# Rotary embedding on one core: cos and sin loaded by SyncE into 32 partitions and spread by TensorE

## The chip, the core and the metric

The kernel runs on one core of one Trainium2 chip. The metric is the device time of one execution in microseconds, as the median over runs. The core's engines are TensorE (PE; its weight loads are PEld), VectorE (DVE), ScalarE (ACT), GpSimd (POOL) and SyncE (SP). Sixteen DMA engines move the data. ScalarE issues DMAs on one hardware queue (q10 in the profile) and SyncE on another (q1).

## What is computed

```python
batch, seq, dim = (16, 512, 1024); num_heads = 16      # head_dim 64, half_dim 32
x = x.reshape(batch, seq, num_heads, head_dim)
x1, x2 = x[..., :half_dim], x[..., half_dim:]
cos = cos[None, :, None, :]; sin = sin[None, :, None, :]    # each (512, 32) float32
out = concatenate([x1 * cos - x2 * sin, x1 * sin + x2 * cos], axis=-1)
```

Everything is float32. x and the output are 33.55 MB each, and each of the two tables is 64 KB.

## The kernel before, in words

**Tiles.** The sixteen batches are cut into ten tiles. Batches 0, 1, 14 and 15 are "singles": partition s holds the sequence rows 4s to 4s+3, 16 KB (R1 = 4). The other twelve go in six pairs: a batch lies in 64 partitions of 8 rows each, 32 KB (R2 = 8). A "row" u is one sequence position per partition, 128 x 1024 elements; there are 64 of them. `x_sb` is a ring of 40 rows; a result is written over its x and stored from there.

**Tables.** A single needs cos and sin with partition s holding positions 4s to 4s+3; a pair needs partition p holding eight positions of its own batch, a different layout. Before, ScalarE issues the loads of both tables (L174) right after the first x load; each is 128 partitions by 512 B and lands in `stage`. From there three things are made. VectorE copies cos to PSUM (L264, `c1_ps`). ScalarE writes sine with both signs to `s1_sb` (L182, L183). For the pairs ScalarE makes a selection matrix `pick` from the identity (L177), two TensorE matmuls with it spread both tables into `pair_ps` (L208), and ScalarE writes signed sine from there to `s2_sb` (L186, L187); VectorE keeps signed sine of one row in PSUM (L271, L272).

**A row's work.** GpSimd multiplies the row, halves swapped, with signed sine into `t2_sb` (L257); for one row in eight of a pair tile VectorE does that instead (L286). VectorE multiplies the row with cos into one of three PSUM slots (L293). The sum is made by VectorE (L304), or, for the rows marked `PE2`, by TensorE adding `t2` through the identity into the PSUM slot (L224), after which ScalarE copies it back (L191). GpSimd also builds the identity at the start (L235, L237); VectorE and TensorE zero the PSUM slots first (L262, L201).

**Order.** Each engine runs a list written out by hand, with semaphores between the lists. ScalarE issues all x loads: those of the first 40 rows at once, later ones between its copies, each after the store that frees its place in the ring (line 194). SyncE issues the stores, a tile at a time (L161). GpSimd's first multiplication waits for `sem_s` (signed sine) and for the first tile; VectorE's first waits for cos, the zeroing and the first tile. Before the pair tiles (`(t, r) == (2, 0)`, row 8) both wait for the second count of `sem_s`.

Of the kernel before, what the change touches and what calls it, by code (L numbers as in the profile page):

```python
# [6 lines left out]
def bass_split_heads_rope_kernel(  # L7
# [18 lines left out]
    HD = dim // H  # L26
    HALF = HD // 2
    P = 128
    R1 = seq // P
# [3 lines left out]
    fp32 = mybir.dt.float32  # L33
# [3 lines left out]
    COPY = mybir.ActivationFunctionType.Copy  # L37
# [24 lines left out]
    NT2 = 6  # L62
    BANK = 512
    EH = H * HD // BANK
    LEAD = 1
    LAG = 10

    with ExitStack() as stack:
        x_sb = stack.enter_context(nc.sbuf_tensor([P, RING, H, 2, HALF], fp32))
        t2_sb = stack.enter_context(nc.sbuf_tensor([P, NT2, H, 2, HALF], fp32))  # L70
        stage = stack.enter_context(nc.sbuf_tensor([P, 2, R1 * HALF], fp32))
        s1_sb = stack.enter_context(nc.sbuf_tensor([P, R1, 2, HALF], fp32))
        s2_sb = stack.enter_context(nc.sbuf_tensor([P, R2, 2, HALF], fp32))
        ident = stack.enter_context(nc.sbuf_tensor([P, P], fp32))
        pick = stack.enter_context(nc.sbuf_tensor([P, 2, P // 2, 2], fp32))
        zero = stack.enter_context(nc.sbuf_tensor([P, BANK], bf16))
        tab_ps = stack.enter_context(nc.psum_tensor([P, BANK], fp32))
        pair_ps = stack.enter_context(nc.psum_tensor([P, 2, 2, R1, HALF], fp32))
# [4 lines left out]
        sem_cos = stack.enter_context(nc.semaphore("cos"))  # L83
        sem_sin = stack.enter_context(nc.semaphore("sin"))
        sem_c = stack.enter_context(nc.semaphore("ctab"))
        sem_s = stack.enter_context(nc.semaphore("stab"))
        sem_z = stack.enter_context(nc.semaphore("zero"))
        sem_i = stack.enter_context(nc.semaphore("ident"))
# [6 lines left out]
        sem_t = stack.enter_context(nc.semaphore("pairs"))  # L95
        sem_a = stack.enter_context(nc.semaphore("act"))

        c1_ps = tab_ps[:, 0:R1 * HALF].rearrange("p (r d) -> p r d", d=HALF)
        v_ps = tab_ps[:, R1 * HALF:R1 * HALF + HD].rearrange("p (t d) -> p t d", d=HALF)

        def c_of(t, r):
            return c1_ps[:, r, :] if tiles[t][1] == R1 else pair_ps[:, r // R1, 0, r % R1, :]
# [50 lines left out]
            eng.dma_start(in_sbuf(t), in_dram(x1, x2, t)).then_inc(sem_in[t], 16)  # L153

        def on_sync(sp):
            for u in range(NU):
                t, r, k = where(u)
                if r == tiles[t][1] - 1:
                    wait_added(sp, u)
                    k = u // R2  # L160
                    sp.dma_start(in_dram(o1, o2, t), in_sbuf(t)).then_inc(sem_out[k] if k < EARLY else sem_rest, 16)  # L161
            sp.wait_ge(sem_rest, 16 * sum(stores_of(k) for k in range(EARLY, NU // R2)))

        def on_scalar(ae):
            later = {}
            for t, (b, n) in enumerate(tiles):
                if b * R1 + n <= RING:
                    load(ae, t)
                else:

                    later.setdefault((b * R1 - RING) // R2 * R2 + R2 - 1 + LAG, []).append(t)
                if t == 0:
                    for i, (table, sem) in enumerate(((cos, sem_cos), (sin, sem_sin))):
                        ae.dma_start(stage[:, i, :], table.rearrange("(s r) d -> s (r d)", r=R1)).then_inc(sem, 16)  # L174

            ae.wait_ge(sem_i, 2)
            ae.activation(  # L177
                pick[:], ident[:].rearrange("q (s k) -> q k s", k=2)[:, :, :, None].broadcast_to([P, 2, P // 2, 2]), COPY
            ).then_inc(sem_g, 1)
            ae.wait_ge(sem_sin, 16)  # L180
            sv = stage[:, 1, :].rearrange("s (r d) -> s r d", d=HALF)
            ae.activation(s1_sb[:, :, 0, :], sv, COPY, scale=-1.0)  # L182
            ae.activation(s1_sb[:, :, 1, :], sv, COPY).then_inc(sem_s, 1)  # L183
            ae.wait_ge(sem_t, 2)
            s2 = s2_sb[:].rearrange("p (k r) t d -> p k r t d", r=R1)
            ae.activation(s2[:, :, :, 0, :], pair_ps[:, :, 1, :, :], COPY, scale=-1.0)  # L186
            ae.activation(s2[:, :, :, 1, :], pair_ps[:, :, 1, :, :], COPY).then_inc(sem_s, 1)  # L187
            for u in range(NU):
                if PE2[u]:
                    ae.wait_ge(sem_e, n_pe[u])  # L190
                    ae.activation(xs[:, u % RING, :], t1_ps[:, u % NT1, :], COPY).then_inc(sem_a, 1)  # L191
                for t in later.get(u, ()):
                    k = (tiles[t][0] * R1 - RING) // R2
                    ae.wait_ge(sem_out[k], 16 * stores_of(k))
                    load(ae, t)

        def on_tensor(pe):
            pe.wait_ge(sem_z, 1)
            for k in range(NT1):
                for b in range(EH):  # L200
                    pe.matmul(  # L201
                        t1_ps[:, k, b * BANK:(b + 1) * BANK], zero[:, 0:P], zero[:], start=True, stop=True
                    ).then_inc(sem_w, 1)
            pe.wait_ge(sem_g, 1)
            pe.wait_ge(sem_cos, 16)
            pe.wait_ge(sem_sin, 16)
            for k in range(2):
                pe.matmul(  # L208
                    pair_ps[:, k].rearrange("p c r d -> p (c r d)"),
                    pick[:, k].rearrange("q s b -> q (s b)"),  # L210
                    stage[:].rearrange("q c f -> q (c f)"),
                    start=True,
                    stop=True,
                ).then_inc(sem_t, 1)
            for u in range(NU):
                if not PE2[u]:
                    continue
                pe.wait_ge(sem_m, u + 1)

                if not V2[u]:  # L220
                    pe.wait_ge(sem_p, n_pool[u])
                t2 = t2_sb[:, u % NT2, :, :, :].rearrange("p h t d -> p (h t d)")
                for b in range(EH):
                    ins = pe.matmul(  # L224
                        t1_ps[:, u % NT1, b * BANK:(b + 1) * BANK],
                        ident[:],
                        t2[:, b * BANK:(b + 1) * BANK],
                        start=False,
                        stop=True,
                        skip_group_check=True,  # L230
                    )
                ins.then_inc(sem_e, 1)

        def on_gpsimd(pl):
            pl.memset(ident[:], 1.0).then_inc(sem_i, 1)  # L235
            pl.wait_ge(sem_i, 1)
            pl.affine_select(  # L237
                out=ident[:],
                in_=ident[:],
                compare_op=mybir.AluOpType.is_equal,  # L240
                fill=0.0,
                base=0,
                pattern=[[-1, P]],
                channel_multiplier=1,
            ).then_inc(sem_i, 1)
            for u in range(NU):
                if V2[u]:
                    continue
                t, r, k = where(u)
                if (t, r) == (0, 0):  # L250
                    pl.wait_ge(sem_s, 1)
                if (t, r) == (2, 0):
                    pl.wait_ge(sem_s, 2)
                if r == 0:
                    pl.wait_ge(sem_in[t], 16)
                wait_t2_free(pl, u)
                pl.tensor_tensor(  # L257
                    t2_sb[:, u % NT2, :, :, :], swapped(k), over_heads(s_of(t, r)), mult
                ).then_inc(sem_p, 1)

        def on_vector(ve):
            ve.memset(zero[:], 0.0).then_inc(sem_z, 1)  # L262
            ve.wait_ge(sem_cos, 16)
            ve.tensor_copy(c1_ps, stage[:, 0, :].rearrange("s (r d) -> s r d", d=HALF)).then_inc(sem_c, 1)  # L264
            ve.wait_ge(sem_c, 1)
            ve.wait_ge(sem_w, NT1 * EH)

            def pair_tables():
# [7 lines left out]
            def mul(u):  # L276
                t, r, k = where(u)
                if r == 0:
                    ve.wait_ge(sem_in[t], 16)
                if (t, r) == (2, 0):  # L280
                    pair_tables()
                if u == first_v:
                    ve.wait_ge(sem_c, 3)
                if V2[u]:
                    wait_t2_free(ve, u)
                    ve.tensor_tensor(t2_sb[:, u % NT2, :, :, :], swapped(k), over_heads(v_ps), mult)  # L286
                if u >= NT1:
                    v = u - NT1
                    if PE2[v]:
                        ve.wait_ge(sem_a, n_pe[v])  # L290
                    else:
                        ve.wait_ge(sem_v, n_comb[v])
                ve.tensor_tensor(  # L293
                    t1_ps[:, u % NT1, :].rearrange("p (h d) -> p h d", d=HALF),
                    x_sb[:, k, :, :, :].rearrange("p h t d -> p (h t) d"),
                    c_of(t, r)[:, None, :].broadcast_to([P, 2 * H, HALF]),
                    mult,
                ).then_inc(sem_m, 1)
# [56 lines left out]
```

## Time and profile before

| What | Value |
|---|---|
| Runs (median of 3) | 161.54 us (161.30 to 161.64) |
| Profiled execution, first to last instruction (span) | 160.3 us |
| Median of the runs less that span | 1.2 us |
| Busy: GpSimd, VectorE, TensorE, ScalarE | 134.9, 130.3, 72.8, 24.4 us |
| DMA: bytes, mean rate over the span | 67.26 MB, 419 GB/s |
| Tables: issue to landing, cos and sin | 7.8 and 7.5 us |
| First x load: issue, issue to landing | 0.81 us, 8.0 us |
| First multiplications: VectorE, GpSimd | 9.37 us, 9.85 us |

For the profiled execution no time is given beside its span; what lies around the span is taken as the difference in the third row. How to read the views: the page's slices cut the span in 40 parts, each digit a busy share in tenths. A queue's share is the time that its packets took, out of 16 engines over the stretch asked for; it can pass 100% when packets overlap or run past the stretch, since a packet counts where it starts. The chain lists start, length and what was waited for; the list of waits has engine and operation, what it waited for, total, times and longest.

### The profile page before, as it was taken

The numbers are of one execution on the slowest core, as the hardware profiler recorded it, in microseconds if no ns is written. First come the engines' busy times: TensorE is split into PE (matmuls) and PEld (weight loads), VectorE is DVE, ScalarE is ACT, GpSimd is POOL, SyncE is SP. The second block draws the span as 40 slices with busy tenths as digits, with TensorE's granted clock in tenths as the row PEclk, the third lists the DMA queues.
The fourth block names the chain that finished last, engine by engine and source line by source line (L and its number), as shares of the span: only waits on it lengthen the run. The fifth ranks groups of instructions, "written<-read, shape, count | busy, mean of one in ns | idle before, by whom it ended". The sixth has DMA issues, their size and how long they took to land.

```text
span 160.3 us, 522 instructions
## 1 busy us (share of the span) xinstructions
PE 72.8 (45%) x94; PEld 24.0 (15%) x94; DVE 130.3 (81%) x117; ACT 24.4 (15%) x27; POOL 134.9 (84%) x64
## 2 busy tenths in 40 slices
PE   6050004478357936660847105489458435850000
PEld 1020002022202211210221002022202111220000
DVE  0069998599989999996999709899889999999500
ACT  0420000203120222022012010201220402040000
POOL 1059999999999999999999999699999999289400
PEclk9955555557755587689687965555555977699555
DMA  5999999999999999999999999999999999999896
GB/s 147 409 441 474 409 450 409 425 429 429 446 429 458 417 411 466 409 433 401 450 433 425 425 409 458 409 433 433 411 429 462 441 417 401 450 441 441 376 450 294
DMA packets 3170, 67.26 MB, mean 419 GB/s; under 512 B 352, under 2 KB 608, under 8 KB 608
## 3 DMA queue, kind: packets, MB, share of 16 engines
q10 hardware_dynamic: 1728, 33.69, 49.6%
q1 hardware_dynamic: 1440, 33.56, 48.9%
q14 instruction: 2, 0.02, 0.0%
HBM read 33.69 MB, written 33.55 MB: 419 GB/s over the span
## 4 chain that ended last, share of the span: by engine, by line
DMA 60%; POOL 13%; DVE 8%; PE 7%; issue 3%; ACT 2%; ACTq 1%; DVEq 0%
DMA x_sb<-in_x_dram 41%; DMA out_dram<-x_sb 18%; POOL t_sb L257 13%; PE t_ps L224 7%; DVE t_ps L293 5%; DVE x_sb L304 3%; ACT x_sb L191 2%; ACTq L153 1%; ACTq L174 1%; DVE t_sb L286 0%; DVEq L303 0%
## 5 line engine op out<-in xcount | busy, mean ns | idle before, releaser
L257 POOL TENSOR_TENSOR t_sb<-x_sb,s_sb 128x1024 f32<-128x1024 f32 x58 | 134.2, 2346 | 14.8 <-ACT s_sb L183 8.5
L224 PE MATMUL t_ps<-t_sb,ident 128*128 128x512 f32 x84 | 68.0, 957 | 63.0 <-DVE t_ps L293 39.2
L293 DVE TENSOR_TENSOR t_ps<-x_sb,pair_ps 128x1024 f32<-128x1024 f32 x48 | 57.7, 1223 | 9.9 <-ACT x_sb L191 9.8
L304 DVE TENSOR_TENSOR x_sb<-t_ps,t_sb 128x1024 f32<-128x1024 f32 x43 | 52.4, 1218 | 2.6 <-POOL t_sb L257 2.6
L224 PEld LDWEIGHTS t_ps<-t_sb,ident 128*128 128x128 f32 x84 | 22.1, 290 | 108.9 <-DVE t_ps L293 74.6
L191 ACT ACTIVATE x_sb<-t_ps 128x1024 f32<-128x1024 f32 x21 | 21.5, 1023 | 109.9 <-PE t_ps L224 96.9
L293 DVE TENSOR_TENSOR t_ps<-x_sb,tab_ps 128x1024 f32<-128x1024 f32 x16 | 19.3, 1222 | 0.1
L286 DVE TENSOR_TENSOR t_sb<-x_sb,tab_ps 128x1024 f32<-128x1024 f32 x6 | 7.3, 1213 | 0.0
L264 DVE COPY tab_ps<-stage 128x128 f32<-128x128 f32 x1 | 0.3, 294 | 7.8 <-DMA stage<-in_cos_dram 7.8
L208 PE MATMUL pair_ps<-stage,pick 128*128 128x256 f32 x4 | 2.0, 667 | 5.4 <-DMA stage<-in_sin_dram 5.4
L201 PE MATMUL t_ps<-zero 128*128 128x512 bf16 x6 | 2.7, 627 | 1.3 <-DVE zero L262 1.3
L208 PEld LDWEIGHTS pair_ps<-stage,pick 128*128 128x128 f32 x4 | 1.2, 324 | 6.4 <-issue 6.3
L177 ACT ACT_TABLE_LOAD x1 | 1.3, 1283 | 5.5 <-issue 5.5
L201 PEld LDWEIGHTS t_ps<-zero 128*128 128x128 bf16 x6 | 0.7, 136 | 2.4 <-DVE zero L262 1.2
L262 DVE MEMSET zero<- 128x256 uint32 x1 | 0.3, 272 | 0.9 <-PEq L337 0.9
L186 ACT ACTIVATE s_sb<-pair_ps 128x256 f32<-128x256 f32 x1 | 0.4, 383 | 1.7 <-PE pair_ps L208 1.7
L182 ACT ACTIVATE s_sb<-stage 128x128 f32<-128x128 f32 x1 | 0.3, 309 | 2.1 <-DMA stage<-in_sin_dram 2.1
L235 POOL MEMSET ident<- 128x128 f32 x1 | 0.2, 204 | 0.3 <-POOLq L337 0.3
L177 ACT ACTIVATE pick<-ident 128x256 f32<-128x256 f32 x1 | 0.4, 416 | 0.0
L187 ACT ACTIVATE s_sb<-pair_ps 128x256 f32<-128x256 f32 x1 | 0.4, 379 | 0.0
L237 POOL TENSOR_SCALAR_AFFINE_SELECT ident<-ident 128x128 f32<-128x128 f32 x1 | 0.3, 292 | 0.1
L337 POOL MEMSET const-float32-0.0<- 128x1 f32 x1 | 0.1, 98 | 0.3 <-issue 0.3
(6 smaller groups left out, 1.0 us busy)
## 6 DMA issues: line engine op xcount, KB each, us to landing
x_sb<-in_x_dram ACTq DMA_DIRECT2D x6, 4096.0 KB, 38.0
out_dram<-x_sb SPq DMA_DIRECT2D x6, 4096.0 KB, 25.0
x_sb<-in_x_dram ACTq DMA_DIRECT2D x4, 2048.0 KB, 22.6
out_dram<-x_sb SPq DMA_DIRECT2D x4, 2048.0 KB, 15.2
stage<-in_cos_dram ACTq DMA_DIRECT2D x1, 64.0 KB, 7.8
stage<-in_sin_dram ACTq DMA_DIRECT2D x1, 64.0 KB, 7.5
```

The costliest lines, as they stand in the source:

```text
L153: eng.dma_start(in_sbuf(t), in_dram(x1, x2, t)).then_inc(sem_in[t], 16)
L174: ae.dma_start(stage[:, i, :], table.rearrange("(s r) d -> s (r d)", r=R1)).then_inc(sem, 16)
L177: ae.activation(pick[:], ident[:].rearrange("q (s k) -> q k s", k=2)[:, :, :, None].broadcast_to([P, 2, P // 2, 2]), COPY).then_inc(sem_g, 1)
L186: ae.activation(s2[:, :, :, 0, :], pair_ps[:, :, 1, :, :], COPY, scale=-1.0)
L191: ae.activation(xs[:, u % RING, :], t1_ps[:, u % NT1, :], COPY).then_inc(sem_a, 1)
L201: pe.matmul(t1_ps[:, k, b * BANK:(b + 1) * BANK], zero[:, 0:P], zero[:], start=True, stop=True).then_inc(sem_w, 1)
L208: pe.matmul(pair_ps[:, k].rearrange("p c r d -> p (c r d)"), pick[:, k].rearrange("q s b -> q (s b)"), stage[:].rearrange("q c f -> q (c f)"),
L224: ins = pe.matmul(t1_ps[:, u % NT1, b * BANK:(b + 1) * BANK], ident[:], t2[:, b * BANK:(b + 1) * BANK], start=False, stop=True, skip_group ...
L257: pl.tensor_tensor(t2_sb[:, u % NT2, :, :, :], swapped(k), over_heads(s_of(t, r)), mult).then_inc(sem_p, 1)
L286: ve.tensor_tensor(t2_sb[:, u % NT2, :, :, :], swapped(k), over_heads(v_ps), mult)
L293: ve.tensor_tensor(t1_ps[:, u % NT1, :].rearrange("p (h d) -> p h d", d=HALF), x_sb[:, k, :, :, :].rearrange("p h t d -> p (h t) d"), c_of ...
L304: ve.tensor_tensor(xs[:, k, :], t1_ps[:, u % NT1, :], t2_sb[:, u % NT2, :, :, :].rearrange("p h t d -> p (h t d)"), add,).then_inc(sem_v, 1)
```

## The change

SyncE's list now begins with the loads of both tables, each into 32 partitions with 2 KB (sixteen positions) per partition; ScalarE no longer issues them. GpSimd builds two sets of selection matrices at the start, `pick1` (32 x 4 x 128) and `pick2` (32 x 2 x 128), with a memset and an affine selection each; these stand ahead of the identity's own selection, which is kept. TensorE spreads the tables by matmuls over 32 rows: four, accumulated, put cos and sin for the singles side by side in the PSUM bank `tab_ps`; two and two do the same for the pairs into `pair_ps` (TQ = 32, TJ = 4, TI = 2, NF = R1 * HALF = 128). VectorE's copy of cos and ScalarE's making of `pick` are gone. ScalarE reads sine for the singles from PSUM, after the new semaphore `sem_f`. VectorE's first work waits for the first count of `sem_s`, which covers the cos table as well, instead of for cos.

```diff
-        stage = stack.enter_context(nc.sbuf_tensor([P, 2, R1 * HALF], fp32))
+        stage = stack.enter_context(nc.sbuf_tensor([TQ, 2, TJ, R1 * HALF], fp32))
-        pick = stack.enter_context(nc.sbuf_tensor([P, 2, P // 2, 2], fp32))
+        pick1 = stack.enter_context(nc.sbuf_tensor([TQ, TJ, P], fp32))
+        pick2 = stack.enter_context(nc.sbuf_tensor([TQ, TI, P // 2, 2], fp32))
...
         def on_sync(sp):
+            for i, (table, sem) in enumerate(((cos, sem_cos), (sin, sem_sin))):
+                sp.dma_start(
+                    stage[:, i].rearrange("q j f -> q (j f)"), table.rearrange("(q n) d -> q (n d)", q=TQ)
+                ).then_inc(sem, 16)
...
         def on_scalar(ae):
-                if t == 0:
-                    for i, (table, sem) in enumerate(((cos, sem_cos), (sin, sem_sin))):
-                        ae.dma_start(stage[:, i, :], table.rearrange("(s r) d -> s (r d)", r=R1)).then_inc(sem, 16)
-
-            ae.wait_ge(sem_i, 2)
-            ae.activation(
-                pick[:], ident[:].rearrange("q (s k) -> q k s", k=2)[:, :, :, None].broadcast_to([P, 2, P // 2, 2]), COPY
-            ).then_inc(sem_g, 1)
-            ae.wait_ge(sem_sin, 16)
-            sv = stage[:, 1, :].rearrange("s (r d) -> s r d", d=HALF)
-            ae.activation(s1_sb[:, :, 0, :], sv, COPY, scale=-1.0)
-            ae.activation(s1_sb[:, :, 1, :], sv, COPY).then_inc(sem_s, 1)
+            ae.wait_ge(sem_f, 1)
+            ae.activation(s1_sb[:, :, 0, :], sin1_ps, COPY, scale=-1.0)
+            ae.activation(s1_sb[:, :, 1, :], sin1_ps, COPY).then_inc(sem_s, 1)
...
         def on_tensor(pe):
-            pe.wait_ge(sem_g, 1)
+            pe.wait_ge(sem_g, 4)
             pe.wait_ge(sem_cos, 16)
             pe.wait_ge(sem_sin, 16)
+            for j in range(TJ):
+                ins = pe.matmul(
+                    tab_ps[:, 0:2 * NF].rearrange("p (c f) -> p c f", c=2),
+                    pick1[:, j],
+                    stage[:, :, j, :],
+                    start=j == 0,
+                    stop=j == TJ - 1,
+                )
+            ins.then_inc(sem_f, 1)
             for k in range(2):
-                pe.matmul(
-                    pair_ps[:, k].rearrange("p c r d -> p (c r d)"),
-                    pick[:, k].rearrange("q s b -> q (s b)"),
-                    stage[:].rearrange("q c f -> q (c f)"),
-                    start=True,
-                    stop=True,
-                ).then_inc(sem_t, 1)
+                for i in range(TI):
+                    ins = pe.matmul(
+                        pair_ps[:, k].rearrange("p c r d -> p c (r d)"),
+                        pick2[:, i].rearrange("q s b -> q (s b)"),
+                        stage[:, :, 2 * i + k, :],
+                        start=i == 0,
+                        stop=i == TI - 1,
+                    )
+                ins.then_inc(sem_t, 1)
...
         def on_gpsimd(pl):
+            pl.memset(pick1[:], 1.0).then_inc(sem_g, 1)
+            pl.memset(pick2[:], 1.0).then_inc(sem_g, 1)
             pl.memset(ident[:], 1.0).then_inc(sem_i, 1)
+            pl.wait_ge(sem_g, 2)
+            pl.affine_select(
+                out=pick1[:],
...
+                pattern=[[-1, TJ], [1, P]],
+                channel_multiplier=-TJ,
+            ).then_inc(sem_g, 1)
+            pl.affine_select(
+                out=pick2[:],
...
+                pattern=[[-1, TI], [1, P // 2], [0, 2]],
+                channel_multiplier=-TI,
+            ).then_inc(sem_g, 1)
             pl.wait_ge(sem_i, 1)
...
         def on_vector(ve):
             ve.memset(zero[:], 0.0).then_inc(sem_z, 1)
-            ve.wait_ge(sem_cos, 16)
-            ve.tensor_copy(c1_ps, stage[:, 0, :].rearrange("s (r d) -> s r d", d=HALF)).then_inc(sem_c, 1)
-            ve.wait_ge(sem_c, 1)
+            ve.wait_ge(sem_s, 1)
             ve.wait_ge(sem_w, NT1 * EH)
...
-                    ve.wait_ge(sem_c, 3)
+                    ve.wait_ge(sem_c, 2)
```

More of the change, by code (lines that the diff above doesn't have):

```diff
@@ L64, in bass_split_heads_rope_kernel @@
     EH = H * HD // BANK
+    TQ = 32
+    TJ = P // TQ
+    TI = TJ // 2
     LEAD = 1
@@ L85, in bass_split_heads_rope_kernel @@
         sem_c = stack.enter_context(nc.semaphore("ctab"))
+        sem_f = stack.enter_context(nc.semaphore("firsttab"))
         sem_s = stack.enter_context(nc.semaphore("stab"))
@@ L96, in bass_split_heads_rope_kernel @@
         sem_a = stack.enter_context(nc.semaphore("act"))
-        c1_ps = tab_ps[:, 0:R1 * HALF].rearrange("p (r d) -> p r d", d=HALF)
-        v_ps = tab_ps[:, R1 * HALF:R1 * HALF + HD].rearrange("p (t d) -> p t d", d=HALF)
+        NF = R1 * HALF
+        c1_ps = tab_ps[:, 0:NF].rearrange("p (r d) -> p r d", d=HALF)
+        sin1_ps = tab_ps[:, NF:2 * NF].rearrange("p (r d) -> p r d", d=HALF)
+        v_ps = tab_ps[:, 2 * NF:2 * NF + HD].rearrange("p (t d) -> p t d", d=HALF)
         def c_of(t, r):
@@ L234, in on_gpsimd @@
         def on_gpsimd(pl):
+            pl.memset(pick1[:], 1.0).then_inc(sem_g, 1)
+            pl.memset(pick2[:], 1.0).then_inc(sem_g, 1)
             pl.memset(ident[:], 1.0).then_inc(sem_i, 1)
+            pl.wait_ge(sem_g, 2)
+            pl.affine_select(
+                out=pick1[:],
+                in_=pick1[:],
+                compare_op=mybir.AluOpType.is_equal,
+                fill=0.0,
+                base=0,
+                pattern=[[-1, TJ], [1, P]],
[3 more added lines that the diff above has]
+                out=pick2[:],
+                in_=pick2[:],
+                compare_op=mybir.AluOpType.is_equal,
+                fill=0.0,
+                base=0,
+                pattern=[[-1, TI], [1, P // 2], [0, 2]],
+                channel_multiplier=-TI,
+            ).then_inc(sem_g, 1)
             pl.wait_ge(sem_i, 1)
```

## The prediction

> **What bounds the kernel now.** I read the page first: the DMA slices and the two queues.
>
> ```profile
> span 160.3 us, 522 instructions
> ...
> DMA  5999999999999999999999999999999999999896
> ...
> q10 hardware_dynamic: 1728, 33.69, 49.6%
> q1 hardware_dynamic: 1440, 33.56, 48.9%
> ```
>
> The shares of the load queue (q10) and the store queue (q1) add up to 98.5% of 16 engines over the span. GpSimd at 84% and VectorE at 81% come after. To see where the missing 1.5% lies, I asked the DMA view for the stretch from 3.3 to 158 us.
>
> ```profile
> DMA packets 3104, 66.44 MB, mean 429 GB/s; under 512 B 336, under 2 KB 592, under 8 KB 592
> ...
> q10 hardware_dynamic: 1706, 33.33, 50.4%
> q1 hardware_dynamic: 1396, 33.10, 50.0%
> ```
>
> Together 100.4%: in this stretch no engine rests. A change to the tables can move the end only through the time that packets occupy engines, or through the ends of the span. The beginning, from the table of windows (PE, weight load, VectorE, ScalarE and GpSimd busy time, then granted clock, DMA share, GB/s):
>
> ```profile
> 0.00:1.80 1.80, 0.55 (x2) 0.28 (x3) 0.27 (x1) 0.00 (x0) 0.70 (x6) 1.00 0.00 0
> 1.80:2.40 0.60, 0.60 (x3) 0.15 (x2) 0.00 (x0) 0.00 (x0) 0.00 (x0) 1.00 1.73 355
> 2.40:3.00 0.60, 0.60 (x3) 0.21 (x2) 0.00 (x0) 0.00 (x0) 0.00 (x0) 1.00 0.43 109
> 3.00:3.60 0.60, 0.60 (x3) 0.08 (x1) 0.00 (x0) 0.00 (x0) 0.00 (x0) 1.00 0.81 273
> 3.60:4.20 0.60, 0.39 (x1) 0.00 (x0) 0.00 (x0) 0.00 (x0) 0.00 (x0) 1.00 0.97 410
> ```
>
> No data until 1.8 us, 1.0 us after ScalarE's first issue at 0.81. In the next 2.4 us 0.6 x (355 + 109 + 273 + 410) = 688 KB start, where 429 GB/s would give 1030 KB: the ramp loses 342 KB, 0.8 us of full rate. Then 1.8 + 0.8 + 67.26 MB at 429 GB/s (156.8) = 159.4 us, and 0.9 us is left for uneven engines and the last completion. That is the whole span.
>
> Is the end set by compute after all? The chain and GpSimd's list of waits:
>
> ```profile
> 93.45 47.51 DMA x_sb<-in_x_dram
> 140.96 0.07 issue
> 141.02 9.29 POOL t_sb L257 x4
> ```
>
> ```profile
> POOL t_sb L257 <- ACT s_sb L183: 8.5, 1, 8.5
> POOL t_sb L257 <- DMA x_sb<-in_x_dram: 4.3, 2, 3.9
> ```
>
> The timeline has the last store issued at 151.70, and it lands at 160.3: 8.6 us, where its own 2.1 MB take 4.9. Some 3.7 us of older stores lie ahead of it, less 1.0 us from issue to data: compute may end 2.7 us later before the end moves. GpSimd waits 3.9 us for the last load besides.
>
> **The change, part by part.** All times are against the 160.3 us span; the median of the runs, 161.54, is 1.24 above it, and I carry this over unchanged.
>
> *Old table packets.* Two DMA windows give their price, the first with 16 KB packets alone, the second with the tables in it:
>
> ```profile
> DMA packets 52, 0.85 MB, mean 426 GB/s; under 512 B 0, under 2 KB 0, under 8 KB 0
> ...
> q10 hardware_dynamic: 52, 0.85, 100.1%
> ```
>
> ```profile
> DMA packets 335, 0.64 MB, mean 399 GB/s; under 512 B 48, under 2 KB 304, under 8 KB 304
> ...
> q10 hardware_dynamic: 335, 0.64, 102.7%
> ```
>
> First, 5 to 7 us: 1.001 x 32 engine-us over 52 packets is 616 ns for 16 KB. Second, 7.4 to 9 us: 1.027 x 25.6 = 26.3 engine-us; 335 - 304 = 31 packets of 16 KB take 19.1 of it; 7.2 are left, over 304 - 48 = 256 rows of 512 B: 28 ns each at most. Every engine carries 16 of them: 0.45 us leave the saturated stretch.
>
> *New table packets.* 64 of 2 KB, 4 for each engine if evenly spread. By bytes from the 16 KB row a 2 KB packet takes 616/8 = 77 ns; with what a 512 B packet has above its bytes (28 - 19 = 9 ns) it takes 86: 0.31 to 0.34 us. Upper bound: four old rows in each, 112 ns, 0.45 us. Lower bound: nothing, if they pass while the engines wait in the ramp, which loses 0.8 us. I take 0.33, between the two prices from 16 KB, since no row shows that the ramp has room in the engines themselves. Sum: -0.45 + 0.33 = -0.12 us.
>
> [...]
>
> *First x load.* In ScalarE's queue it was and stays first, at 0.81; nothing moves if the two queues are served side by side. SyncE's two issues (0.46 and 0.45 on ScalarE) fall into SyncE's 19.7 us wait for the first store; nobody waits behind them. Bounds of what they do to the load: 0 to 0.46 + 0.03 + 0.45 = 0.94 us later, if served first. I take 0: data came 1.0 us after the issue with the next issues already under way. A gain isn't excluded either: if the table packets meet the ramp's slowness in place of the 16 KB ones, part of the 0.8 comes back.
>
> *Second x load.* It is issued at about 1.21 instead of 2.17. Its packets are wanted when the first load's 2.1 MB have gone, at 1.8 + 0.8 + 4.9 = 7.5 us: 5 us of cover, worth nothing. If that cover were gone, it would gain the 0.96.
>
> *GpSimd* gains two memsets and two selections. The memset row (128 elements, 204 ns, against 98 ns for one element) gives 0.52 and 0.31; the selection (292 ns for 128), between fixed and proportional, 0.29 to 1.17 and 0.29 to 0.58. At most 0.82 + 0.41 + 1.17 + 0.58 = 3.0 us if all is proportional. It starts at 0.80, so the picks are ready by about 4.0, and GpSimd idles to 9.85: hidden. Without that cover the selections would cost up to 3.0.
>
> *TensorE.* The zeroing ends at 3.99 as before. The old two table matmuls (4 records) took from 9.37 to 11.42, 2.05 us at a granted clock of 0.5. Four for the first tables are 8 records: 4.1 us, half of that at best, if the clock of 1.0 that the windows show here counts in full. They wait for the tables: landing at 4 or so if served beside the first load, at 9.0 (as now) if behind it. ScalarE's pick copy (0.42) and VectorE's table copy (0.29) go; ScalarE's two sine copies stay (0.50 from 9.26), now behind TensorE. VectorE and GpSimd get their tables at 4.0 + 4.1 + 0.5 + 0.1 = 8.7 us, or 9.0 + 4.7 = 13.7. The first load lands 8.0 us after its issue, at 8.8. So GpSimd starts between 1.0 us earlier (8.8 for 9.85) and 3.9 us later. Queued behind VectorE's new wait is its first multiplication, and the first store after that; loads for 40 ring rows (21 MB, 49 us) keep the engines full meanwhile. 3.9 us later is just GpSimd's wait for the last load. Price 0; if GpSimd's slack and the 2.7 us at the end were both gone, each later us would cost one.
>
> *Pair tables.* Four more matmuls, 4.1 us, ready by 13.7 + 4.8 = 18.5 at worst (with both ScalarE copies); VectorE first reads them at 26.11. Hidden.
>
> Total: 161.54 - 0.12 = 161.42.
>
> **The rivals.** *Slower: the tables go ahead of the first load.* SyncE is free as early as ScalarE; if the 64 rows are prepared first, the large load starts up to 0.94 us later and the table packets pass in that gap. Price +0.94 - 0.45 = +0.49: 162.03. It is slower by over 0.2% once the first x data come more than 0.45 + 0.32 = 0.77 us later, near 2.6. For it: the rate falls to 109 GB/s right after the first burst, so the start is touchy. Against it: the x load is issued no later than now.
>
> *Faster: the ramp swallows the tables.* Engines at 109 to 273 GB/s between 2.4 and 3.6 have 0.8 us to give; then the 0.45 us are all gained: 161.09, and 160.9 if a quarter of the ramp's loss comes back too. For it: 2 KB is small beside what is lost. Against it: the DMA share, 1.73 in the first window, counts those slow packets as occupying their engines.
>
> *The tables are not spread as assumed.* If the 32 rows fall on 8 engines, these carry 8 packets, 0.65 us, and the slowest engine sets the end: +0.20, 161.74. For it: 32 rows is a new shape. Against it: the old shape loaded all engines alike.
>
> **How the numbers follow.** Forecast 0.41, with its own range 161.2 to 161.6; slower rival 0.26; ramp rival 0.25; uneven spread 0.08. About 0.2% (0.32 us) is what a measurement of this kernel can tell from no change; the runs shown lie 0.34 apart. Faster: 0.25 + 0.06 from the forecast's lower edge = 0.31. Slower: 0.24 of the first rival's 0.26, 0.02 of the uneven spread, 0.02 of the forecast = 0.28. The rest is 0.41. The range reaches to the ramp rival's lower price and just past the first rival's, 160.9 to 162.1.
>
> **What the next profile should show.** Right: 64 packets of 2 KB on q1 before 5 us; first data at 1.8; 429 GB/s and 100% from about 3.3 us on; tables landed near 4 us, GpSimd's first multiplication at 8.7 to 10. Wrong: x data that start past 2.6 us, a longer stretch below 410 GB/s, any slice below 9 between 4 and 156 us, or GpSimd starting after 13.7 us and the last store being issued past 154.4.

## The result, and the profile after

The changed kernel takes 162.90 us (median of 5 runs, 162.34 to 163.31) against 161.61 for the kernel before: ratio 1.0081, with a 95% interval of 1.0057 to 1.0106. Measured again beside the experiments below, it was 162.44 against 161.31: 1.0060 (1.0039 to 1.0081). Medians here are over all runs; the ratios leave out single executions over 1.5% above the fastest of the same kernel, and are not the quotients of the medians. The forecast was 161.42 with a range of 160.9 to 162.1; slower by over 0.2% had been given 0.28.

The profiled execution took 163.31 us in all, of which 161.2 are the span: 2.1 us lie outside it. In the second measurement every run of both kernels has the two numbers. The kernel before has a median span of 159.9 and 1.42 outside (23 runs, 1.38 to 1.47); the changed kernel has a span of 160.3 and 2.04 outside (5 runs, 1.84 to 2.47). So of 1.1 us, 0.4 lie inside the span and 0.6 outside it, where the forecast had put no change.

The page's DMA slices and queues after:

```profile
span 161.2 us, 548 instructions
...
DMA  5999999999999999999999999999999999999994
...
q1 hardware_dynamic: 1536, 33.69, 49.0%
q10 hardware_dynamic: 1440, 33.56, 48.8%
```

The engines are as full as before, and the tables have gone over to q1. The DMA view from 3.3 to 158 us says the same:

```profile
DMA packets 2895, 66.57 MB, mean 430 GB/s; under 512 B 332, under 2 KB 332, under 8 KB 372
...
q10 hardware_dynamic: 1427, 33.34, 50.3%
q1 hardware_dynamic: 1466, 33.21, 49.9%
```

430 GB/s for 429: between 3.3 and 158 us the DMA engines work as fast as before. The beginning, in the same windows as before:

```profile
1.80:2.40 0.60, 0.60 (x3) 0.17 (x2) 0.00 (x0) 0.00 (x0) 0.60 (x2) 1.00 1.23 195
2.40:3.00 0.60, 0.60 (x3) 0.21 (x2) 0.00 (x0) 0.00 (x0) 0.60 (x1) 1.00 0.96 133
3.00:3.60 0.60, 0.60 (x3) 0.09 (x1) 0.00 (x0) 0.00 (x0) 0.60 (x2) 1.00 0.46 164
3.60:4.20 0.60, 0.40 (x1) 0.00 (x0) 0.00 (x0) 0.00 (x0) 0.24 (x1) 1.00 0.98 410
```

0.6 x (195 + 133 + 164 + 410) = 541 KB start by 4.2 us, against 688 before: at 429 GB/s the ramp takes 0.34 us more. Other traces agree: 541 KB in the repeat (`changed_again`) and 509 in `changed_short_list`, which has the same loads, against 672 and 673 in two runs with the loads of the kernel before (`spare_buffer_only`, `late_same_list`). Then the tables' path, from the timeline:

```profile
9.31 3.75 PE L211 MATMUL tab_ps<-stage,pick 32*128 32x256 f32 x8 [5.31 <-DMA stage<-in_sin_dram]
...
13.09 0.28 ACT L185 ACTIVATE s_sb<-tab_ps 128x128 f32<-128x128 f32 x1 [7.24 <-PE tab_ps L211]
...
13.57 2.36 DVE L325 TENSOR_TENSOR t_ps<-x_sb,tab_ps 128x1024 f32<-128x1024 f32 x2 [12.37 <-ACT s_sb L186]
13.62 9.27 POOL L291 TENSOR_TENSOR t_sb<-x_sb,s_sb 128x1024 f32<-128x1024 f32 x4 [9.78 <-ACT s_sb L186]
```

In brackets stands how long the engine was idle and for what. Sine lands at 9.2 us, TensorE spreads the tables until 13.06, and both multipliers start at 13.6 instead of 9.4 and 9.85. The page's DMA issues show that it is the second table that is late:

```profile
stage<-in_cos_dram SPq DMA_DIRECT2D x1, 64.0 KB, 4.2
stage<-in_sin_dram SPq DMA_DIRECT2D x1, 64.0 KB, 7.9
```

Last, what lies behind the span. The DMA view from 161 to 165 us, where the kernel before has no packet at all:

```profile
DMA packets 1, 0.02 MB, mean 4 GB/s; under 512 B 0, under 2 KB 0, under 8 KB 0
## 3 DMA queue, kind: packets, MB, share of 16 engines
q8 instruction: 1, 0.02, 1.7%
```

One packet of instructions, 16 KB on a queue of its own (1.7% of 16 engines over 4 us: 1.1 us), begins more than a microsecond after the kernel's last instruction. The trace has it from 162.52 to 163.61 us.

### The profile page after: what moved, and what is told of

Its sections match the earlier page's. It is cut to its first block, busy times and chain, and to the rows that moved or that the text cites. A ratio compares the mean times of both kernels' runs of the same rounds, so it can differ in the third digit from the quotient of the medians.

```text
span 161.2 us, 548 instructions
## 1 busy us (share of the span) xinstructions
PE 75.7 (47%) x106; PEld 27.4 (17%) x106; DVE 129.8 (81%) x116; ACT 23.9 (15%) x26; POOL 137.2 (85%) x68
## 4 chain that ended last, share of the span: by engine, by line
DMA 32%; DVE 17%; POOL 16%; PE 14%; issue 9%; ACT 4%; ACTq 1%; DVEq 0%; POOLq 0%
DMA out_dram<-x_sb 18%; POOL t_sb L291 16%; DMA x_sb<-in_x_dram 14%; PE t_ps L237 14%; DVE t_ps L325 9%; DVE x_sb L336 6%; ACT x_sb L194 4%; DVE t_sb L318 2%; ACTq L160 1%; POOLq L153 0%; DVEq L322 0%; DVEq L335 0%
## 5 line engine op out<-in xcount | busy, mean ns | idle before, releaser
L291 POOL TENSOR_TENSOR t_sb<-x_sb,s_sb 128x1024 f32<-128x1024 f32 x58 | 134.0, 2352 | 9.8 <-ACT s_sb L186 9.8
L237 PE MATMUL t_ps<-t_sb,ident 128*128 128x512 f32 x84 | 65.8, 933 | 62.4 <-DVE t_ps L325 38.2
L237 PEld LDWEIGHTS t_ps<-t_sb,ident 128*128 128x128 f32 x84 | 21.5, 282 | 106.4 <-DVE t_ps L325 68.5
L211 PE MATMUL tab_ps<-stage,pick 32*128 32x256 f32 x8 | 3.7, 646 | 5.3 <-DMA stage<-in_sin_dram 5.3
L211 PEld LDWEIGHTS tab_ps<-stage,pick 32*128 32x128 f32 x8 | 2.5, 327 | 6.7 <-issue 6.2
L221 PE MATMUL pair_ps<-stage,pick 32*128 32x256 f32 x8 | 3.6, 629 | 0.0
L221 PEld LDWEIGHTS pair_ps<-stage,pick 32*128 32x128 f32 x8 | 2.7, 333 | 0.7
L261 POOL TENSOR_SCALAR_AFFINE_SELECT pick<-pick 32x256 f32<-32x256 f32 x1 | 1.2, 1247 | 0.0
L248 POOL MEMSET pick<- 32x512 f32 x1 | 0.5, 514 | 0.3 <-POOLq L369 0.3
L252 POOL TENSOR_SCALAR_AFFINE_SELECT pick<-pick 32x512 f32<-32x512 f32 x1 | 0.6, 627 | 0.0
```

The lines of the kernel that those rows point to most:

```text
L211: ins = pe.matmul(tab_ps[:, 0:2 * NF].rearrange("p (c f) -> p c f", c=2), pick1[:, j], stage[:, :, j, :], start=j == 0, stop=j == TJ - 1,)
L221: ins = pe.matmul(pair_ps[:, k].rearrange("p c r d -> p c (r d)"), pick2[:, i].rearrange("q s b -> q (s b)"), stage[:, :, 2 * i + k, :], s ...
L237: ins = pe.matmul(t1_ps[:, u % NT1, b * BANK:(b + 1) * BANK], ident[:], t2[:, b * BANK:(b + 1) * BANK], start=False, stop=True, skip_group ...
L261: pl.affine_select(out=pick2[:], in_=pick2[:], compare_op=mybir.AluOpType.is_equal, fill=0.0, base=0, pattern=[[-1, TI], [1, P // 2], [0, 2]],
L291: pl.tensor_tensor(t2_sb[:, u % NT2, :, :, :], swapped(k), over_heads(s_of(t, r)), mult).then_inc(sem_p, 1)
```

## Experiments on TensorE's list

After the prediction three theories stood against each other at first. A: the table packets in the ramp hold up the first x load, and an engine that is held up stays behind. B: the later start of compute costs, against the forecast's price of 0. C: the end and the time outside the span come from the larger program. The first runs narrowed C to TensorE's list (theory D).

**Twelve matmuls added where nothing waits for them** (`longer_pe_list`).

```diff
             pe.wait_ge(sem_z, 1)
+            for k in range(12):
+                pe.matmul(t1_ps[:, 0, 0:P], zero[:, 0:P], zero[:, 0:P], start=True, stop=True)
```

> The kernel before with twelve short zeroing matmuls (128 columns) added ahead of TensorE's others; they run while it would idle, nothing starts later. The three slow kernels so far have 106 matmul and 106 weight-load records (before: 94 and 94), a 16 KB packet on queue 8 after their span, and 1.9 to 2.2 us outside the span (before 1.2). Theory B (late start alone): 161.4, span 160.2. Theory D (a longer TensorE list costs time outside the span, as a second part of the loss): the 16 KB packet appears, the span stays, and the time rises by 0.6 to 0.8 us to 162.1.

161.82 against 161.32: ratio 1.0036 (1.0019 to 1.0053), although VectorE and GpSimd start no later (9.17 and 9.61). The page's queues:

```profile
q10 hardware_dynamic: 1728, 33.69, 49.5%
q1 hardware_dynamic: 1440, 33.56, 48.6%
q8 instruction: 1, 0.02, 0.0%
```

The packet is there, at 130 us this time, inside the span. Its price moved with it: span 160.5 (before 159.9), outside 1.24 (before 1.42). The packet came with the longer list and the time rose, as the theory had it; the place was not as it had it, for it left the span unchanged. How a packet at 130 us would lengthen the span by 0.6 us isn't shown. One reading, a guess of mine, is that its 0.93 us are work for one of the sixteen DMA engines, and that this engine then finishes last and sets the end. The table of windows from 159.0 to 159.5 us seems to fit, the kernel before first, then this one (last columns: DMA share and GB/s of packets that start there):

```profile
159.00:159.50 0.50, 0.00 (x0) 0.00 (x0) 0.00 (x0) 0.00 (x0) 0.00 (x0) 0.50 0.69 295
```

```profile
159.00:159.50 0.50, 0.00 (x0) 0.00 (x0) 0.00 (x0) 0.00 (x0) 0.00 (x0) 0.50 0.08 33
```

A share of 0.69 of 16 engines over 0.5 us is 5.5 engine-us, nine last packets of 0.61; 0.08 is a single one. But `spare_buffer_only`, which has no packet of instructions on queue 8 and takes as long as the kernel before (0.9992), ends in the same way:

```profile
159.00:159.50 0.50, 0.00 (x0) 0.00 (x0) 0.00 (x0) 0.00 (x0) 0.00 (x0) 0.50 0.09 33
```

So a lone last packet is no sign of the longer list, and this reading stays a guess.

**The changed kernel with TensorE's old number of matmuls** (`changed_again` for comparison, `changed_short_list`).

```diff
-    PE2 = [R1 <= u < NU - R1 and u % R2 in (1, 3, 6) for u in range(NU)]
+    PE2 = [R1 <= u < NU - R1 and u % R2 in (1, 3, 6) and u not in (22, 38, 54) for u in range(NU)]
```

> The changed kernel as it is, for spans and time outside them on one chip with the next three. If an instruction packet of 16 KB on queue 8 is the largest part (theory D): 2.0 us outside the span against 1.4 of the kernel before, and a span 0.4 to 0.8 longer; 162.5 to 162.9. If only the late start counted (theory B), the time outside would be that of before.

> The changed kernel with three rows (22, 38, 54) added by VectorE instead of TensorE and ScalarE: TensorE's list has 94 matmul records again, as before the change; VectorE has three additions more, GpSimd and the start are as in the changed kernel. Theory D: no packet on queue 8, 1.4 us outside the span, so 0.6 less than the changed kernel, near 162.1. Theory B alone: as the changed kernel.

The changed kernel came out at 162.44; with 94 matmul records it is 161.81, ratio 1.0028 (1.0013 to 1.0043) to the kernel before. No packet of instructions follows the span: the DMA view from 160 to 166 us holds a single packet on q1, of under 512 B.

```profile
DMA packets 1, 0.00 MB, mean 0 GB/s; under 512 B 1, under 2 KB 1, under 8 KB 1
## 3 DMA queue, kind: packets, MB, share of 16 engines
q1 hardware_dynamic: 1, 0.00, 0.0%
```

Outside the span there are 1.24 us instead of 2.04; the span is 160.6 against 160.3, with three more additions on VectorE. The net gain, 0.63 us, is the part that was foreseen. The span has a loss of its own here: the windows from 139 to 141 us show a gap that the changed kernel doesn't have (1.10 in `changed_again`):

```profile
139.00:141.00 2.00, 1.26 (x2) 0.75 (x3) 2.00 (x3) 0.00 (x0) 2.00 (x2) 0.50 0.65 279
```

The traces also tie the measured time to the packet. Where the packet follows the span, its end, counted from the span's start, lies 0.3 us behind the time that the same execution took, although the packet's length varies:

| Kernel | Length of the packet | Packet ends | Execution took |
|---|---|---|---|
| the changed kernel | 1.09 us | 163.61 us | 163.31 us |
| `changed_again` | 1.08 us | 162.68 us | 162.37 us |
| `scalar_new_shape` | 0.95 us | 162.54 us | 162.24 us |
| `late_compute` | 1.22 us | 163.34 us | 163.04 us |

So in these four executions the measured time goes with the packet's end, 0.30 to 0.31 us short of it, and not with the last store; where the constant 0.3 us comes from isn't shown. Without a packet behind the span, about 1.24 or 1.42 us lie outside it in the median of a kernel's runs, and what makes it the one or the other isn't known either.

**Fewer matmuls by larger pieces** (`sixty_four_rows`).

```diff
-    TQ = 32
+    TQ = 64
```

> The changed kernel with 64 rows of 1 KB for each table: two and two matmuls spread them (98 records in all, before 94, changed 106), and compute starts some 2 us earlier than in the changed kernel. Theory D: if 98 records still fit, no packet, 1.4 us outside, 161.7 to 162; if not, 162.3. Theory B alone: half of the loss, 162.1. Theory A: the ramp is as in the changed kernel.

161.95, ratio 1.0033 (1.0019 to 1.0048). With 98 records there is no packet and 1.42 us outside; a number between 98 and 106 was not run. The earlier start did not come: sine, in 64 rows of 1 KB, landed at 12.5 us, later than in 32 rows, and GpSimd began at 15.28. What went with this start can be seen in the table of windows from 139 to 141 us, the kernel before first, then this one:

```profile
139.00:141.00 2.00, 1.89 (x3) 0.50 (x2) 2.00 (x3) 0.85 (x1) 0.00 (x0) 0.55 1.18 508
```

```profile
139.00:141.00 2.00, 0.60 (x1) 0.50 (x2) 2.00 (x3) 0.00 (x0) 2.00 (x2) 0.50 0.69 295
```

The last two columns are DMA share and GB/s: 0.69 and 295, in the middle of what had been a full stretch. The loads are done, and the next store isn't there yet: the last packet of a load ends at 134.0 us and the store is issued at 139.3; before, the load's last packet ends at 139.3 and the store is issued at 135.6.

## Experiments on the late start and on the ramp

**Only the start moved, by more matmuls** (`late_compute`): six table matmuls ahead of the old ones, and both first multiplications behind them.

```diff
+            for k in (0, 1) * 3:
+                pe.matmul(pair_ps[:, k] ..., pick[:, k] ..., stage ...).then_inc(sem_f, 1)
...
             ae.wait_ge(sem_sin, 16)
+            ae.wait_ge(sem_f, 6)
...
+            ve.wait_ge(sem_s, 1)
             ve.wait_ge(sem_w, NT1 * EH)
```

> The kernel before with six extra table matmuls (repeats of the pairs') ahead of its own; signed sine and cos are held until they are done, so that VectorE and GpSimd start some 3 us later; DMAs are as before. Theory A: 161.6, since GpSimd's slack of 3.9 us covers it. Theory B: 162.5 to 163. Theory C: 161.6.

163.09, ratio 1.0091 (1.0058 to 1.0125), with the start at 14.78: as much as the whole change. I read this first as theory B alone. But the kernel has 106 matmul records too, its packet of instructions follows the span (2.25 us outside in the profiled execution), and only about half of the loss is the start. In its span the same gap as above is to be seen:

```profile
139.00:141.00 2.00, 0.73 (x1) 0.50 (x2) 2.00 (x3) 0.00 (x0) 2.00 (x2) 0.66 0.69 295
```

**Only the start moved, with no work added** (`late_same_list`): ScalarE's sine copies in another order, and one wait more in VectorE's list.

```diff
-            ae.activation(s1_sb[:, :, 0, :], sv, COPY, scale=-1.0)
-            ae.activation(s1_sb[:, :, 1, :], sv, COPY).then_inc(sem_s, 1)
             ae.wait_ge(sem_t, 2)
             ae.activation(s2[:, :, :, 0, :], pair_ps[:, :, 1, :, :], COPY, scale=-1.0)
             ae.activation(s2[:, :, :, 1, :], pair_ps[:, :, 1, :, :], COPY).then_inc(sem_s, 1)
+            ae.activation(s1_sb[:, :, 0, :], sv, COPY, scale=-1.0)
+            ae.activation(s1_sb[:, :, 1, :], sv, COPY).then_inc(sem_s, 1)
...
-                    pl.wait_ge(sem_s, 1)
+                    pl.wait_ge(sem_s, 2)
...
+            ve.wait_ge(sem_s, 2)
             ve.wait_ge(sem_w, NT1 * EH)
```

> The kernel before with ScalarE's four sine copies in another order: the pairs' two first, the singles' two last, and VectorE's and GpSimd's first work behind them. No instruction is added; both start at some 12.5 us (before: 9.4 and 9.85). Theory B: half a microsecond to one slower than before, 161.9 to 162.4, with gaps in the DMA engines' work after 134 us. Theory D alone: 161.4, and no packet on queue 8.

161.66, ratio 1.0019 (1.0003 to 1.0034), start at 12.8, no packet, 1.42 us outside. The late start costs, but 0.3 us (0.05 to 0.55 by the interval), not the 0.5 to 1 that was expected; and the trace shows no gap at 134 us or after. The whole is in the span, whose median is 160.25 for 159.9.

**SyncE issues the tables in the old shape** (`sync_old_shape`), and the same with VectorE held until sine is ready (`sync_old_shape_late`).

```diff
         def on_sync(sp):
+            for i, (table, sem) in enumerate(((cos, sem_cos), (sin, sem_sin))):
+                sp.dma_start(stage[:, i, :], table.rearrange("(s r) d -> s (r d)", r=R1)).then_inc(sem, 16)
```

> The kernel before, but SyncE issues both tables first, in the old shape (128 rows of 512 B); ScalarE no longer does. Theory A (the table packets meet the DMA engines' cold start ahead of the first x load, and one engine that is held up there stays behind to the end): about the changed kernel's loss, 162.5 to 163, with x packets that start near 3.7 us on many engines. Theory B (the later start of compute, 13.6 us instead of 9.8, costs): the sine table is used 0.5 us after it lands, with no matmul between, so 161.6 or a little under. Theory C (the new tail and the time outside the span come from the larger program): 161.6.

> The kernel with SyncE issuing the tables in the old shape, and VectorE's first work held as well until signed sine is ready, as in the changed kernel: both start near 12.2 us, 94 matmul records. Theory B (late start) with theory A: the sum of the two, 161.7 to 162.1 (as the changed kernel without its instruction packet). If VectorE's start alone decides: 161.5.

161.49, ratio 1.0020 (1.0004 to 1.0036); with VectorE held as well 161.71, ratio 1.0029 (1.0013 to 1.0046). Theory A's 162.5 is refuted. In this shape sine lands at 11.7 us, 10.4 after its issue, so GpSimd starts at 12.3 even without a matmul between. The second kernel has neither the new shape nor TensorE's spreading, and yet a median span of 160.25 us, nearly the changed kernel's 160.3. Its start is late and its ramp is slow as well (557 KB by 4.2 us), so it doesn't tell the two apart.

**ScalarE issues the new shape after the first x load** (`scalar_new_shape`).

```diff
         def on_sync(sp):
-            for i, (table, sem) in enumerate(((cos, sem_cos), (sin, sem_sin))):
...
         def on_scalar(ae):
+                if t == 0:
+                    for i, (table, sem) in enumerate(((cos, sem_cos), (sin, sem_sin))):
+                        ae.dma_start(stage[:, i] ..., table.rearrange("(q n) d -> q (n d)", q=TQ)).then_inc(sem, 16)
```

> The changed kernel, but ScalarE issues the two 32-row table loads after the first x load, as before. Theory A: back to 161.5 (161.4 by the packets' price). Theory B: compute starts at 13.6 or later still, so 162.9 or more. Theory C: 162.9, and 2 us outside the span as in the changed kernel.

162.25, ratio 1.0053 (1.0033 to 1.0073). Theory A wanted 161.5. The list is as long as in the changed kernel: in most of its runs about 2 us lie outside the span (median 1.99), and the span is 160.35. Putting the loads back brings back next to nothing, though the ramp is whole again (672 KB by 4.2 us). Its start is later still (14.55 us for GpSimd), so the late start and the ramp aren't told apart here either.

**The tables ahead of everything, in ScalarE's queue**, in the changed kernel with the new shape (`new_tables_ahead`) and in the kernel before with the old (`old_tables_ahead`, whose edit is shown).

```diff
         def on_scalar(ae):
+            for i, (table, sem) in enumerate(((cos, sem_cos), (sin, sem_sin))):
+                ae.dma_start(stage[:, i, :], table.rearrange("(s r) d -> s (r d)", r=R1)).then_inc(sem, 16)
             later = {}
```

> The changed kernel, but ScalarE issues the two 32-row table loads, ahead of the first x load in the same queue. Tables land near 3.5 us, TensorE spreads them by about 8.2, and compute starts as soon as the first x load is there, near 9.2. Theory B alone: all of the loss is gone, 161.3. Theory D: the start is as early, but the list is as long as in the changed kernel: 162.0, with the packet on queue 8.

> The kernel before, but ScalarE issues the two tables (old shape) ahead of the first x load instead of behind it. VectorE and GpSimd both start when the first x load is there, near 9.2 instead of 9.4 and 9.85. Theory B: 161.2 to 161.4 (a gain of up to 0.2, if the start counts below 9.8 us as well). Theory A (packets in the ramp): 161.8 or more.

162.64, ratio 1.0083 (1.0054 to 1.0111), and 162.03, ratio 1.0038 (1.0024 to 1.0051). Neither theory alone gives the first: compute starts at 9.6 us and the loss is as large as the change's. The difference of the two, 0.6 us, goes with the packet of instructions, which comes at 142 us here. In three of the eight runs 1.6 to 2.1 us lie outside the span, in the others 1.2; where the packet came in the seven without a trace isn't known. The second shows what a real delay of the first x load costs: it is issued at 1.70 instead of 0.81, lands at 9.6 instead of 8.8, and the kernel loses 0.6 us; its table packets don't make up for that.

**The tables after the zeroing** (`sync_after_zeroing`).

```diff
         def on_sync(sp):
+            sp.wait_ge(sem_w, NT1 * EH)
```

> The changed kernel, but SyncE issues the tables only when TensorE has zeroed its slots, at 4.0 us, when the first x load is in full flow. Theory A: the first x packets start at 1.8 us again and 161.5 follows, though compute starts at 14 us or later. Theory B: 163 or more. Theory C: 162.9.

163.76, ratio 1.0135 (1.0105 to 1.0164), the slowest of the variants of the change itself; it also has the long list. It speaks for B and D and against A. How far its start moved in these runs isn't known.

**The tables a second time, into a buffer that nobody reads**: from SyncE in the new shape (`spare_new_shape`), in the old shape (`spare_old_shape`), from ScalarE behind the first x load (`spare_from_scalar`), and the buffer alone (`spare_buffer_only`).

```diff
+        spare = stack.enter_context(nc.sbuf_tensor([32, 2, P * R1 * HALF // 32], fp32))
...
         def on_sync(sp):
+            for i, table in enumerate((cos, sin)):
+                sp.dma_start(spare[:, i, :], table.rearrange("(q n) d -> q (n d)", q=32)).then_inc(sem_x, 16)
```

> The kernel before, and SyncE loads both tables besides, first of all and in the new shape (32 rows of 2 KB), into a buffer that nobody reads; all else as before. It has the ramp of the change without its late start and longer list. Theory A: the time of the packets (0.33 us) and more, 162.0 or above, with the slowest engine over 1.2 us behind the fastest. Otherwise 161.4 to 161.7: the packets alone.

> The kernel before, and SyncE loads both tables besides, first of all, into a spare buffer in the old shape (128 rows of 512 B). Theory A for any packets among the first x packets: 163 to 164, as with the new shape. If the new shape's 2 KB rows into 32 partitions do the harm: 161.6 to 161.9, the price of the packets (0.45) and little else.

> The kernel before, and ScalarE loads both tables in the new shape besides, behind the first x load, ahead of its own table loads. If SyncE's queue at the start does the harm: 161.6 to 161.8 (0.33 us of packets, and compute some 0.3 us later). If the new shape does: 163 or more.

> The kernel before with the spare buffer (4 KB in 32 partitions) allocated and never loaded: the identity, the selection and the zeros lie 4 KB higher. If the 2.5 us came from the loads: 161.3. If from where the buffers lie: 163.8.

Ratios 1.0140 (1.0106 to 1.0174), 1.0100 (1.0083 to 1.0118), 1.0105 (1.0067 to 1.0144) and 0.9992 (0.9981 to 1.0004). These were meant to measure the ramp by itself, and failed as such. In both shapes from SyncE, and in the new one from ScalarE, two extra loads of 64 KB cost 1.6 to 2.3 us, where the forecast's prices for such packets are 0.3 to 0.45. In the first of them the loss isn't in the ramp alone: the DMA view from 60 to 140 us gives 425 GB/s, where the kernel before has 429.

```profile
DMA packets 1300, 33.97 MB, mean 425 GB/s; under 512 B 138, under 2 KB 138, under 8 KB 138
```

That is 0.9% of 80 us, 0.7 us, of the 3.2 us by which this trace's span is longer. Why two loads at the start should slow the middle isn't settled. For the question here it says only that 32 rows of 2 KB are no special evil: the old shape, and ScalarE's queue, did about the same.

## Why the prediction was wrong, point by point

*What bounds the kernel*: right. The DMA engines are full from 3.3 to 158 us in both kernels, at 429 and 430 GB/s.

*The time outside the span*: this is the step that failed, and the largest. "The median of the runs, 161.54, is 1.24 above it, and I carry this over unchanged." It rose by 0.62 us, half of the loss. Shown by the packet of instructions that the trace has behind the span and 0.3 us short of whose end the measured time ends, by its absence with 94 or 98 matmul records, and by its presence with twelve idle matmuls added. The 1.24 itself was the median of some executions less the span of another; in the later runs of the kernel before that have both numbers, 1.37 to 1.48 us lie outside.

*TensorE*: the forecast costed four and four matmuls by their time and found it covered. The time was right (3.75 us for the first four; 4.1 forecast). That the list itself has a length, and that 106 records don't cost what 94 do, was no term of the sum: the list's growth stood at nothing, without a reason, and the runs put some 0.6 us in its place.

*The start of compute*: its time was bounded rightly, 8.7 to 13.7, and came out at 13.6; the price of 0 did not hold. `late_same_list` gives 0.3 us for 3 us. The reasoning that failed was the slack: GpSimd's wait of 3.9 us for the last load was taken as reserve. With the later start the third store from the end is issued at 136.8 us instead of 135.6, and the loads run ahead: their last packet ends at 139.3 us before, at 136.6 after. After the change GpSimd's list of waits is:

```profile
POOL t_sb L291 <- ACT s_sb L186: 9.8, 1, 9.8
POOL const-float32-0.0 L369 <- issue: 0.3, 1, 0.3
```

The wait for loads is gone, as assumed; but what is late next is the store that should follow when the loads are over. The gap is shown at 139 us, but it goes by the issue of that store rather than by the start. Issued at 139.2 and 139.3 us, with starts at 14.8 and 15.3, it leaves a DMA share of 0.69; at 138.6, with a start at 13.4 and three more additions on VectorE (`changed_short_list`), 0.65. Issued at 138.2 (`scalar_new_shape`, start at 14.55) or before, it leaves none: 1.07 there, and 0.91 and 1.10 in the changed kernel and its repeat, where it is issued at 136.8 and 136.9. So the changed kernel, and `late_same_list` too, lose without a gap, and how those 0.3 us come about stays open: the last 16 KB packet of a store starts at 160.2 us in the changed kernel's trace, but at 159.3 in its repeat, as in the kernel before.

*GpSimd*: hidden, as forecast. The picks are ready at 3.60 us, although the smaller selection took 1.25 us, over its bound of 0.58; the sum of the bounds held because the larger one took 0.63 of 1.17, which is luck.

*The packets*: right for those that pass while the engines are full, and there alone. From 5.5 to 6.6 us of the changed kernel's trace the DMA view counts q1 alone with the tables:

```profile
DMA packets 39, 0.48 MB, mean 438 GB/s; under 512 B 0, under 2 KB 0, under 8 KB 11
...
q10 hardware_dynamic: 28, 0.46, 98.5%
q1 hardware_dynamic: 11, 0.02, 5.3%
```

0.053 x 16 x 1.1 us over 11 packets of 2 KB is 85 ns, within the 77 to 86 of the forecast; an eighth of a 16 KB packet's 616 ns is 77. In `scalar_new_shape`, where all 64 come together between 7.4 and 9.2 us, 45 took 84 ns and the last 19 took 107 to 181; what lengthened those wasn't tested. Half of the 64 packets pass in the ramp, before 5 us, where seven take 1.03 to 1.82 us; all 64 have a mean of 242 ns (240 in the repeat), three times the forecast's 77 to 86, and the sine table lands at 9.2 us, not near 4. The x packets of the ramp are slow too (0.78 us in the mean for the 26 that start before 4 us, 0.61 for most after that), so these durations are no measure of what was lost, but "nothing, if they pass while the engines wait in the ramp" had it the wrong way round: the ramp became longer. The gain of 0.12 is not to be found: the second x load lands, issue plus duration, at 1.24 + 13.4 = 14.6 us, and at 14.3 in the repeat, against 2.17 + 11.9 = 14.1 before and 13.9 to 14.3 in three other runs with the loads of before. All table bytes have passed by then in either kernel, so the change is a few tenths of a us behind at this point. How much of this reaches the end beside the late start can't be told: the 0.4 us inside the span are what `sync_old_shape_late` has as well, with both, and the intervals of these runs are each 0.3% wide.

*The first x load and the slower rival*: not the cause. x data start at 2.05 us and at 2.14 in the repeat, not past 2.6. In `changed_short_list`, with the same loads, they start at 2.67, so the limit that the rival had set is passed in some executions. Where the load is truly second the kernel does lose (`old_tables_ahead`, 0.6 us; the rival's price was 0.49), but in the changed kernel's two traces the packets of both queues start within 0.3 us of each other. The ramp rival was wrong in direction, by the 541 KB above; no view counts packets by engine, so on the uneven spread nothing was shown.

None of the runs beat the kernel before clear of noise.

## What to carry to other kernels

The profile's span was not the time that was measured: 1.2 to 2.5 us lay outside it in the runs here. List what lies around it as a term of the sum, and ask of each engine's list whether the change makes it longer. Lighter packets at the start could gain here at most the time of those that they replace, 0.45 us, and in the ramp even that was lost. GpSimd's wait of 3.9 us at the end was no reserve for a start 3 us later, which cost 0.3 us (`late_same_list`): ask which transfers will then find nothing to do.

## What the runs showed of the hardware

- With 106 matmul records, the traces of the changed kernel, `changed_again`, `scalar_new_shape`, `late_compute`, `longer_pe_list` and `new_tables_ahead` have a packet of instructions of 16 KB; the kernel before and `changed_short_list`, with 94, and `sixty_four_rows`, with 98, don't. It took 0.93 to 1.22 us. Behind the span it comes with about 0.6 us more outside it (2.04 for 1.42), and the measured time ends 0.3 us short of the packet's end, counted from the span's start; inside the span, at 130 us in `longer_pe_list`, it comes with 0.5 us net. Its place differs between two kernels with the same TensorE list (162.5 us in the changed kernel and 142.3 in `new_tables_ahead`); what sets it was not tried.
- In the changed kernel SyncE issues two loads of 64 KB at 0.81 and 1.26 us while ScalarE's queue loads x: in 32 rows the first took 4.2 us from issue to landing, the second 7.9; in 128 rows (`sync_old_shape`) the second took 10.4. Ahead of x in ScalarE's own queue it took 2.0 us in 32 rows (`new_tables_ahead`) and 2.2 in 128 (`old_tables_ahead`).
- TensorE's four table matmuls took 3.75 us from 9.31 in the changed kernel, where the granted clock was 0.5; in `new_tables_ahead`, from 3.93, where it was 1.0, they took 2.10.
- Two extra loads of 64 KB at the start cost 1.6 to 2.3 us in all (`spare_old_shape`, `spare_from_scalar`, `spare_new_shape`), several times the 0.3 to 0.45 at which the forecast put such packets.
